# Hybrid encoder layer on one core: rows of 1 / rms spread inside the chip instead of through memory, the queries' row moved into the attention sigmoid

## The chip, the cores and the metric

The kernel runs on one core of one Trainium2 chip. The metric is the device time of one execution in microseconds (us). The kernel before was run three times: median 2429.84 us, from 2428.33 to 2432.44. The trace of before comes from a further, profiled execution of 2430.59 us.

## The reference, cut to what matters

One layer of a streaming encoder over 2048 prompt tokens and 64 sample tokens, model width 1024. `h = rms_norm(x)` goes through one input projection of 2048 columns. Part of them are queries and keys of 4 heads of 64:

```python
q = rms_norm(q.reshape(B, L, 4, 64), q_norm) * 64 ** -0.5
k = rms_norm(k.reshape(B, L, 4, 64), k_norm)
z = einsum("bqhd,bkhd->bhqk", q, k)              # stick-breaking attention
nl = where(mask, log1p(exp(z)), 0)               # 1 - sigmoid(z) = sigmoid(-z) survives
attn = where(mask, exp(z - surv), 0); o = attn @ v
x = x + concat(y_lru * gelu, y_pool, o) @ w_out
x = x + (silu(h2 @ w_gate) * (h2 @ w_up)) @ w_down    # h2 = rms_norm(x)
```

`rms_norm` multiplies each token (for q and k: each token and head) by one number, 1 / sqrt(mean of squares + eps), and each channel by a weight. The normalised keys are an output; the normalised queries are not.

## The kernel before, in words

The tokens are worked through in four groups of 512 (group 0 takes the 64 sample tokens along). Activations lie transposed: channels on the 128 partitions, tokens along the free axis. Every large product is done with operands split into a high and a low part (three matmuls). The split weights of the input projection are made in group 0, kept in memory (`wk`) and read back in groups 1 to 3.

`X_first` (L815) does the start: it loads x of group 0 and the values' weights, splits both, and computes the values' projection. In group 0 the rms factor is applied after the projection (`leave`, L305), from a tile `rb` in which every partition holds the row of 1 / rms over the tokens. The sums of squares come from matmuls with a column `ones`, which put them on the partitions (token = partition); GpSimd raises them to the power -0.5 (`inv_rms`, L138). To turn this column into a row on all partitions, before writes it to memory (`xrow`, L878) and reads it back broadcast to 128 partitions (L879). The sample tokens have their own write and read (L890, L891).

`QK_parts` (L326) treats one half (two heads, index j) of the queries or keys of one group in three steps: `mm_` projects into `raw` and squares it into `sq`; `ev_` sums the squares per head by matmuls with `sel`, takes the power -0.5 on GpSimd, writes the result to memory (`row`, L353; `rows` for the sample, L361) and reads it back broadcast into `rbk` (L356, L363); `fin_` multiplies `raw` by channel weight and `rbk` on VectorE (L368), splits it into `hl` (L314 on ScalarE, L315 on VectorE) and stores it for the attention (`qscr`, `kscr`). There are 16 such units: 4 groups, queries and keys, two halves. In the attention, `att_qtile` (L647) multiplies queries with keys into `z` and applies sigmoid with the scale -1 (L653), after which VectorE scans (L657, L661).

The order on each engine is set by a scheduler that simulates the program with its own costs; a string of tokens (`o0`, `o1`, `o3`) sets the order in which units are handed to it. Each engine then works strictly in its order, and so does SyncE's queue (SP), which issues every DMA: an issue that waits for a semaphore holds all behind it. `b_rbk` is 1: there is one `rbk` tile. `ps_mm` hands out three PSUM banks.

Of the kernel before, what the change touches and what calls it, by code (L numbers as in the profile page):

```python
# [3 lines left out]
def prm(n,d):  # L4
    return type(d)(PRM.get(n,d))
# [7 lines left out]
F32 = mybir.dt.float32  # L13
F32R = mybir.dt.float32r
# [7 lines left out]
P = 128  # L22
# [27 lines left out]
def hybrid_layer(ctx: ExitStack, tc: tile.TileContext, x_all, x_t, w_in, w_out, w_gu, w_dn, par, gates, poolw,  # L50
# [26 lines left out]
    def mm(out, lhsT, rhs, start, stop):  # L77
        pe.matmul(out, lhsT, rhs, start=start, stop=stop)  # L78
# [12 lines left out]
    qscr = [dram.tile([NH, HD, 2, GW], F32, name=f"qscr{g}") for g in range(NG)]  # L91
    qkrow = [[[dram.tile([2, GW], F32, name=f"row{g}{w}{j}") for j in range(2)] for w in range(2)] for g in range(NG)]
    qkrow_s = [[dram.tile([2, NS], F32, name=f"rows{w}{j}") for j in range(2)] for w in range(2)]
    mix = [dram.tile([KD, P, GW], F32, name=f"mix{g}") for g in range(NG)]
# [69 lines left out]
    def ps_t():  # L164
        return psum.tile([P, 4, P], F32, name="tp", tag="tp", bufs=prm("ntp", 2))
# [23 lines left out]
    qn8 = p1.tile([P, 1], F32, name="qn8")  # L189
    dve.tensor_scalar(qn8, pv("qn"), HD ** -0.5, None, ALU.mult)  # L190
    sel = p1.tile([P, 2], F32, name="sel")
# [113 lines left out]
    def leave(out, ps, g, a):  # L305
# [3 lines left out]
        else:  # L309
            act.copy(out, ps)  # L310

    def qk_split(raw, n):
# [5 lines left out]
    def q_store(hl, n, j, dst):  # L318
        for e in range(2):
            sp.dma_start(dst[2 * j + e], hl[e * HD:e * HD + HD, :, :n].bitcast(F32))  # L320

# [4 lines left out]
    def QK_parts(g, which, j):  # L326
# [11 lines left out]
        def ev_():  # L338
            raw, sq = st["raw"], st["sq"]
            ps = ps_st(prm('stt0', 0) if g == 0 else prm('stt', 0))  # L340
            rs = sm.tile([P, 10], F32, name="rs4")
            rs2 = sm.tile([P, 10], F32, name="rs42")
# [11 lines left out]
            rb = pq.tile([P, WM], F32, name="rbk", bufs=prm("b_rbk", 1))  # L354
            for e in range(2):
                sp.dma_start(rb[e * HD:e * HD + HD, :GW], row[e:e + 1, :].to_broadcast([HD, GW]))  # L356
            W = GW
            if g == 0:
                W = WM
                row = qkrow_s[which][j]  # L360
                sp.dma_start(row.rearrange("h p -> p h"), rs2[:NS, 8:10])  # L361
                for e in range(2):
                    sp.dma_start(rb[e * HD:e * HD + HD, GW:], row[e:e + 1, :].to_broadcast([HD, NS]))  # L363
            st["rb"] = rb, W

        def fin_():
            raw, (rb, W) = st["raw"], st["rb"]
            dve.scalar_tensor_tensor(raw[:, :W], raw[:, :W], qn8 if which == 0 else pv("kn"), rb[:, :W],  # L368
                                     ALU.mult, ALU.mult)
            for (a, n, t0, first) in [(0, GW, g * GW, True)] + ([(GW, NS, SEQ, False)] if g == 0 else []):  # L370
                hl = qk_split(raw[:, a:a + n], n)
                if which == 0:
                    q_store(hl, n, j, qscr[g] if first else qscr_s)
                else:
                    sp.dma_start(new_k[j * P:(j + 1) * P, t0:t0 + n], raw[:, a:a + n])
                    k_store(hl, n, j, kscr[g] if first else kscr_s[:, :, PAST:])

# [268 lines left out]

    def att_qtile(q2, n, K, w, dg, carry):  # L647

# [24 lines left out]
    def ATT_units(g):  # L673
        us = []
        for h in range(NH):
            st = {}
            for c in range(g, -1, -1):
# [11 lines left out]
                def u(pr, h=h, c=c, st=st, ld=ld):  # L689
# [33 lines left out]
    def ATT_sample(h):  # L723
# [9 lines left out]
        av = psum.tile([P, GW], F32, name="av", tag="av", bufs=1)  # L733
        at, _ = att_qtile(q2[:, :, :n], n, K, w, NS, 0.0)
        tp = ps_a()
# [79 lines left out]
    def X_first():  # L815
# [3 lines left out]
        for i in range(4):  # L819
# [10 lines left out]
            else:  # L830
# [5 lines left out]
        sp.dma_start(ident, ident_in)  # L836
        shift_consts()
        acc = [psum.tile([P, 512], F32, name=t, tag=t, bufs=b) for t, b in
               (("tp", prm("ntp", 2)), ("tp", prm("ntp", 2)), ("z", prm("nz", 2)), ("z", prm("nz", 2)), ("av", 1))]
# [28 lines left out]
        ps = ps_mm()  # L868
        rs = []
        rb = px.tile([P, WM], F32, name="rb", bufs=1)  # L870
        for o in (4, 0):
            for c in range(4):
                cs = slice(c * P, c * P + P) if o == 0 else slice(c, GW, 4)
                for e in range(2):
                    mm(ps[:, o + c:o + c + 1], sums[e][:, cs], ones, e == 0, e == 1)
            rs.append(inv_rms(sm, ps[:, o:o + 4], P, 4))
            if o:
# [10 lines left out]
        mm(ps[:NS, 8:9], ssm, ones, True, True)  # L888
        rss = inv_rms(sm, ps[:NS, 8:9], NS, 1)
        sp.dma_start(xrow[0][0:1, GW:].rearrange("o p -> p o"), rss[:NS, 0:1])  # L890
        sp.dma_start(rb[:, GW:], xrow[0][0:1, GW:].to_broadcast([P, NS]))  # L891
        for k in range(KD):
            mm3(acc[4][:NS, :256], hh_[:, k, GW:], hl_[:, k, GW:], W[k][0], W[k][1], k == 0, k == KD - 1)
        rb0.append(rb)
        for j, (ti, c0, n) in enumerate(toks(0)):
            with hp('ev'):
                ev_v(0, acc[j][:, :256], ti, c0, n, rss[:n, 0:1] if j == 4 else rs[1][:, j:j + 1])

# [478 lines left out]
```

## Time and profile before

| | |
|---|---|
| median of 3 runs | 2429.84 us |
| the profiled execution, its own time | 2430.59 us |
| its span, first to last instruction | 2428.8 us |
| TensorE (PE) busy | 2315.6 us, 95% |
| VectorE (DVE) busy | 1561.7 us, 64% |
| GpSimd (POOL) busy | 1112.7 us, 46% |
| ScalarE (ACT) busy | 965.6 us, 40% |
| mean granted TensorE clock | 0.975 of 2.4 GHz |
| PE busy from 1000 us to the end | 1408.05 of 1428.80 us |

The chain that ended last is 72% PE, 12% DVE, 9% DMA. A PE row counts records: a matmul of plain fp32 shows as two. In a timeline a piece has its start, its length, the engine, the line, what it writes and reads, and in brackets the idle time before it and what ended that.

### The profile page before, as it was taken

What the parts mean: (1) busy time and instruction counts of PE and PEld (TensorE: products, weight loads), DVE (VectorE), ACT (ScalarE), POOL (GpSimd) and SP (SyncE); (2) the same over time, 40 slices, a digit from 0 to 9 for tenths busy, and PEclk for the clock granted to TensorE, in tenths of its full rate; (3) what the DMA queues carried; (4) which work ended last, traced back from release to release, by engine and by line L of the source; (5) the groups of instructions that cost most, each with busy time, mean ns of one, the idle gap of its engine ahead of it and who ended that gap; (6) DMA issues with size and microseconds to landing.
All of it is one profiled execution on the core that took longest, in us unless ns stands there. A gap on an engine that the chain in (4) does not pass through costs nothing.

```text
span 2428.8 us, 38577 instructions
## 1 busy us (share of the span) xinstructions
PE 2315.6 (95%) x14230; PEld 2204.5 (91%) x14230; DVE 1561.7 (64%) x2514; ACT 965.6 (40%) x1804; POOL 1112.7 (46%) x818
## 2 busy tenths in 40 slices
PE   6987999999889989889999999999999999999999
PEld 6976778779678989889999999999999999999999
DVE  4568486796798644696676768655554655555455
ACT  4545364464565422233333343334333433333332
POOL 4533030131131133576565666656565765655552
PEclk8999999999999999999999999999999999999999
DMA  8986777656546354774343348633333563333332
GB/s 281 262 280 197 222 219 225 192 192 206 170 150 175 104 146 129 250 233 131 113 139 118 123 147 267 237 105 122 109 108 114 160 214 108 118 112 108 115 110 74
DMA packets 228478, 399.90 MB, mean 165 GB/s; under 512 B 37697, under 2 KB 99714, under 8 KB 220354
## 3 DMA queue, kind: packets, MB, share of 16 engines
q1 hardware_dynamic: 228290, 397.44, 52.6%
q8 instruction: 112, 1.84, 0.3%
q14 instruction: 76, 0.62, 0.1%
HBM read 300.81 MB, written 96.54 MB: 164 GB/s over the span
## 4 chain that ended last, share of the span: by engine, by line
PE 72%; DVE 12%; DMA 9%; issue 3%; ACT 2%; SPq 1%; POOL 1%; DVEq 0%; ACTq 0%; POOLq 0%
PE gu L78 33%; PE dn L78 20%; PE mm L78 14%; PE z L78 2%; PE av L78 2%; DVE C L661 1%; PE tp L705 1%; DMA rb<-xrow 1%; DMA kscr<-hl 1%; PE tp L78 1%; DVE xc L533 1%; DMA rbk<-row 1%; DMA x1all<-xr 1%; DMA wk<-w 1%; DVE al L1226 1%
## 5 line engine op out<-in xcount | busy, mean ns | idle before, releaser
L86 POOL TENSOR_TENSOR w<-x,w 128x512 fp32r<-128x512 f32 x462 | 640.7, 1401 | 509.7 <-ACT w L1103 478.4
L78 PE MATMUL dn<-ah,wd 128*128 128x352 f32 x2112 | 548.0, 324 | 5.4 <-ACT ah L1225 3.4
L78 PE MATMUL gu<-ht,w 128*128 128x352 f32 x2112 | 545.8, 323 | 7.3 <-DVE u L1180 7.1
L1103 ACT CAST w<-x 128x512 fp32r<-128x512 f32 x462 | 279.0, 619 | 521.2 <-PE gu L78 295.8
L78 PE MATMUL mm<-hTh,w 128*128 128x512 f32 (+3 forms) x1632 | 431.2, 342 | 13.7 <-DVE xr L1005 7.3
L78 PE MATMUL gu<-hb,w 128*128 128x352 f32 x1584 | 417.3, 325 | 9.0 <-DMA x<-in_w_gu 7.3
L1256 DVE TENSOR_TENSOR acc<-dn,acc 128x352 f32<-128x352 f32 x528 | 273.1, 522 | 217.5 <-PE dn L78 216.9
L78 PEld LDWEIGHTS dn<-ah,wd 128*128 128x128 f32 x2112 | 376.4, 189 | 7.6 <-ACT ah L1225 4.2
L78 PEld LDWEIGHTS gu<-ht,w 128*128 128x128 f32 x2112 | 375.1, 188 | 8.9 <-issue 5.9
L78 PE MATMUL dn<-al,wd 128*128 128x352 f32 x1056 | 342.4, 324 | 3.3 <-DVE al L1226 3.3
L78 PE MATMUL gu<-lt,w 128*128 128x352 f32 x1056 | 341.0, 323 | 0.0
L78 PEld LDWEIGHTS mm<-hTh,w 128*128 128x128 f32 x1632 | 290.2, 194 | 44.3 <-DVE xr L1005 8.5
L78 PEld LDWEIGHTS gu<-hb,w 128*128 128x128 f32 x1584 | 284.1, 189 | 11.1 <-ACT w L1103 9.5
L78 PE MATMUL mm<-hTl,w 128*128 128x512 f32 (+3 forms) x816 | 277.6, 341 | 0.8 <-DVE hTl L303 0.4
L78 PE MATMUL gu<-lb,w 128*128 128x352 f32 x792 | 257.1, 325 | 0.0
L86 POOL TENSOR_TENSOR wd<-x,wd 128x512 fp32r<-128x512 f32 x132 | 192.4, 1478 | 51.6 <-ACT wd L1244 51.6
L78 PEld LDWEIGHTS dn<-al,wd 128*128 128x128 f32 x1056 | 199.7, 189 | 4.5 <-DVE al L1226 4.5
L78 PEld LDWEIGHTS gu<-lt,w 128*128 128x128 f32 x1056 | 198.6, 188 | 0.0
L78 PEld LDWEIGHTS mm<-hTl,w 128*128 128x128 f32 x816 | 157.8, 193 | 15.7 <-issue 1.4
L661 DVE TENSOR_TENSOR_SCAN C<-z,C,zero 128x512 f32<-128x512 f32 (+4 forms) x148 | 160.6, 1087 | 13.9 <-ACT z L653 7.5
L1180 DVE TENSOR_TENSOR u<-gu,u 128x352 f32<-128x352 f32 x132 | 68.9, 522 | 129.1 <-PE gu L78 128.8
L78 PEld LDWEIGHTS gu<-lb,w 128*128 128x128 f32 x792 | 150.0, 189 | 0.0
(272 smaller groups left out, 3540.5 us busy)
## 6 DMA issues: line engine op xcount, KB each, us to landing
x<-in_w_gu SPq DMA_DIRECT2D x220, 256.0 KB, 3.3
w<-wk SPq DMA_DIRECT2D x46, 1024.0 KB, 5.7
x<-wsc SPq DMA_DIRECT2D x176, 256.0 KB, 3.4
x<-in_w_dn SPq DMA_DIRECT2D x132, 256.0 KB, 2.8
wsc<-x SPq DMA_DIRECT2D x88, 256.0 KB, 2.7
wk<-w SPq DMA_DIRECT2D x16, 1024.0 KB, 9.1
V<-vscr SPq DMA_DIRECT2D x40, 256.0 KB, 3.8
K<-kscr SPq DMA_DIRECT2D x40, 256.0 KB, 3.6
```

Source lines behind the costliest of these rows:

```text
L78: pe.matmul(out, lhsT, rhs, start=start, stop=stop)
L86: gp.tensor_tensor(out, src, hi, ALU.subtract)
L533: dve.scalar_tensor_tensor(xc[:, a:b], xa[:, s + j:s + j + b - a], pv("cw", c * 4 + j), xc[:, a:b], ALU.mult, ALU.add)
L661: dve.tensor_tensor_scan(C[:n, :w][:, ::-1], om[:n, :w][:, ::-1], zero1[:n].to_broadcast([n, w]), carry, ALU.mult, ALU.add)
L705: pe.transpose(tp[:, kt, :], at[:, kt * P:(kt + 1) * P], ident)
L1103: act.copy(w[:, 0, :], src)
L1180: add = lambda o, x, y: dve.tensor_tensor(o, x, y, ALU.add)
L1226: dve.tensor_tensor(al[:, cs], o, ah[:, cs], ALU.subtract)
L1256: dve.tensor_tensor(acc[:, d, a:b], ps[:, :HT], acc[:, d, a:b], ALU.add)
```

## The change

Queries are no longer multiplied by their 1 / rms. The split `hl` of a query is made from `raw` times the channel weight (now with a minus sign) directly; the 1 / rms of the query tokens, which the power leaves on partitions, is kept in the tiles `qrs`, and the attention's sigmoid takes it as a scale per partition instead of the constant -1. Keys and the rms of group 0 still need a row on all partitions: `rows` transposes the 8 columns of 1 / rms on PE to 8 rows, ScalarE copies these to SBUF, and `spread` makes the row on all 128 partitions by four fp32 matmuls with a table of ones and zeros (`pick`), into PSUM, where VectorE reads it for the keys (for group 0, ScalarE copies it into `rb`). The tokens of a sum of squares are taken in blocks of 128 instead of every fourth one. All writes and reads of `row`, `rows` and, for group 0, `xrow` are gone.

```diff
@@ X_first and QK_parts share:
+    def rows(r, smp, tp=None):
+        tp = ps_t().rearrange("p a b -> p (a b)") if tp is None else tp
+        rt = sm.tile([8, P + NS], F32, name="rt", bufs=2)
+        pe.transpose(tp[:8, :P], r[:, :8], ident)
+        act.copy(rt[:, :P], tp[:8, :P])
+        if smp:
+            pe.transpose(tp[:2, P:P + NS], r[:NS, 8:10], ident[:NS, :NS])
+            act.copy(rt[:2, P:], tp[:2, P:P + NS])
+        return rt
+    def spread(rt, ps):
+        for t in range(4):
+            mm(ps[:, t * P:t * P + P], pick[:, t, :], rt[:, :P], True, True)
@@ ev_ of QK_parts
-                mm(ps[:, t:8:4], sq[:, t:GW:4], sel, True, True)
+                mm(ps[:, t:8:4], sq[:, t * P:t * P + P], sel, True, True)
...
-            row = qkrow[g][which][j]
-            sp.dma_start(row.rearrange("h (p t) -> p h t", t=4), rs2[:, :8].rearrange("p (h t) -> p h t", t=4))
...
-                sp.dma_start(rb[e * HD:e * HD + HD, :GW], row[e:e + 1, :].to_broadcast([HD, GW]))
...
+            if which:
+                st["rt"] = rows(rs2, g == 0)
@@ fin_ of QK_parts
-            dve.scalar_tensor_tensor(raw[:, :W], raw[:, :W], qn8 if which == 0 else pv("kn"), rb[:, :W],
-                                     ALU.mult, ALU.mult)
...
+            if which == 0:
...
+                    act.activation(hl[:, 0, :n], r, AF.Copy, scale=qn8)
+                    dve.scalar_tensor_tensor(hl[:, 1, :n], r, qn8, hl[:, 0, :n], ALU.mult, ALU.subtract)
...
+                    ps = ps_mm()
+                    spread(st["rt"], ps)
+                dve.scalar_tensor_tensor(r, r, pv("kn"), ps[:, :n], ALU.mult, ALU.mult)
+                hl = qk_split(r, n)
@@ att_qtile
-        act.activation(om[:n, :w], z[:n, :w], AF.Sigmoid, scale=-1.0)
+        act.activation(om[:n, :w], z[:n, :w], AF.Sigmoid, scale=rs)
@@ X_first
-        for o in (4, 0):
...
-                sp.dma_start(xrow[0][0:1, :GW].rearrange("o (p t) -> (o p) t", t=4), rs[0][:, :4])
-                sp.dma_start(rb[:, :GW], xrow[0][0:1, :GW].to_broadcast([P, GW]))
+        for c in range(4):
+            for e in range(2):
+                mm(ps[:, c:c + 1], sums[e][:, c * P:c * P + P], ones, e == 0, e == 1)
...
+        rbp = ps_mm()
+        spread(rows(rs, False, ps[:, P:]), rbp)
+        act.copy(rb[:, :GW], rbp)
```

How the change moves instructions, at three places. First PE right after the sums of squares in `X_first` (`w_604` and `w_598` are the weights of the first query half; `rsx` is the column of 1 / rms, `rt` its transposed rows). Before:

```order
L78 MATMUL mm<-ones,r 128x1
L78 MATMUL mm<-ones,i 128x1
L78 MATMUL mm<-hTh,w_604 128x288
L78 MATMUL mm<-hTl,w_604 128x288
L78 MATMUL av<-w_247,hTh 64x256 x2
```

Now, some rows further:

```order
L78 MATMUL av<-w_314,hTl 64x256
L326 MATMUL mm<-ident,rsx 8x128
L453 MATMUL tp<-ident,vf 128x128 x4
L78 MATMUL mm<-rt,pick 128x128 x4
L78 MATMUL mm<-ones,ssm 64x1
L78 MATMUL mm<-hTh,w_598 128x288
L78 MATMUL mm<-hTl,w_598 128x288
```

The transposition and the four spreading matmuls now stand ahead of the first query projection, which before stood behind the sums; the second set of sums, which followed it, is gone.

Second, SP's queue around the first query half's row (`row_69`, `rows_85`). Before:

```order
L353 DMA row_69<-rs_730 128x2x4
L361 DMA rows_85<-rs_730 64x2x1
L283 DMA xt<-in_x_all 128x1024 x2
L430 DMA vtscr_95<-vT 128x2x128
L293 DMA xrow_104<-rs_3005 128x4
L446 DMA vf<-in_cache_v 128x256 x2
L223 DMA stg<-in_w_in 128x1024
L409 DMA vscr_61<-vs 128x512
L356 DMA rbk<-row_69 64x512 x2
L363 DMA rbk<-rows_85 64x64 x2
```

Now, at the same place:

```order
L227 DMA stg<-in_w_in 128x1024
L236 DMA wk_0_1049<-w_1044 128x2048
L390 DMA qscr_65<-hl 64x1024 x2
L457 DMA vtscr_75<-vT 128x2x128
L287 DMA xt<-in_x_all 128x1024 x2
```

The write and the reads of the row are gone, and the store of the split query stands where the row's write stood.

Third, PE in group 1 at the keys of group 2 (`pick` again the table, `rs_4151` and `rs_4221` the two halves' columns). Before:

```order
L78 MATMUL mm<-sel,sq 128x2 x4
L78 MATMUL mm<-xc,pw 128x512
L705 MATMUL tp<-ident,C 128x128
L78 MATMUL tp<-vf,dm 128x256
L78 MATMUL tp<-vf,em 128x256
```

Now:

```order
L733 MATMUL tp<-ident,C 128x128 x4
L326 MATMUL tp<-ident,rs_4151 8x128
L78 MATMUL av<-aTh,V 128x256
L733 MATMUL tp<-ident,C 128x128 x4
L78 MATMUL mm<-rt,pick 128x128 x4
L78 MATMUL mm<-xc,pw 128x512
L78 MATMUL mm<-sel,sq 128x2 x4
```

One matmul and four transpositions stand between the transposition of the keys' row and the matmuls that spread it, which need ScalarE's copy of it.

## Rows read from the trace of the kernel before

**Rows 1.** Stages: window, length, busy us PE, PEld, DVE, ACT, POOL; clock; DMA share; GB/s.

```profile
30.00:60.00 30.00, 19.60 (x129) 17.97 (x128) 2.78 (x12) 8.83 (x19) 10.49 (x7) 0.78 0.97 293
90.00:120.00 30.00, 30.00 (x189) 27.65 (x188) 20.79 (x44) 13.68 (x24) 20.27 (x12) 0.94 0.99 258
120.00:150.00 30.00, 23.98 (x136) 21.29 (x136) 19.96 (x37) 13.37 (x22) 9.16 (x6) 0.83 0.85 239
```

**Rows 2.** PE timeline, first stall: start, length, what; idle before it and releaser.

```profile
49.87 0.78 PE L78 MATMUL tp<-vf,dm 128*128 128x256 f32 x2 [3.00 <-ACT vT L428]
53.39 0.66 PE L426 MATMUL tp<-ident,vf 128*128 128x128 f32 x2 [1.89 <-DVE vs L408]
59.56 0.61 PE L78 MATMUL mm<-hTh,w 128*128 128x288 f32 x1 [5.51 <-DVE raw L308]
```

**Rows 3.** SP timeline, group 0's row of 1 / rms, and the chain's piece of it.

```profile
31.27 1.45 SPq L878 DMA_DIRECT2D xrow<-rs  x1
48.64 0.32 SPq L879 DMA_DIRECT2D rb<-xrow  x1
...
48.64 10.39 DMA rb<-xrow
```

**Rows 4.** Stages after two stalls, same columns as rows 1.

```profile
59.50:64.00 4.50, 4.44 (x18) 4.44 (x19) 0.83 (x3) 2.60 (x5) 0.00 (x0) 0.50 1.03 325
130.00:140.00 10.00, 4.46 (x9) 2.78 (x10) 7.90 (x10) 6.52 (x12) 7.00 (x5) 0.61 0.82 255
```

**Rows 5.** DMA in group 0: packets of 104 to 120 us; stages, last columns share and GB/s.

```profile
DMA packets 1675, 2.78 MB, mean 174 GB/s; under 512 B 1036, under 2 KB 1036, under 8 KB 1546
...
60.00:76.00 16.00, 16.00 (x88) 15.50 (x88) 2.94 (x8) 9.84 (x19) 4.66 (x3) 0.77 1.01 362
76.00:87.00 11.00, 11.00 (x83) 10.90 (x82) 4.71 (x11) 5.57 (x12) 4.48 (x3) 1.00 1.04 148
108.00:120.00 12.00, 12.00 (x93) 12.00 (x92) 11.97 (x22) 3.27 (x6) 9.70 (x5) 1.00 0.96 110
```

**Rows 6.** Timelines of DVE (first row) and PE, second stall.

```profile
130.09 2.88 DVE L368 SCALAR_TENSOR_TENSOR raw<-raw,qn,rbk 128x576 f32<-128x576 f32 x1 [6.23 <-DMA rbk<-rows]
133.38 1.33 PE L78 MATMUL mm<-xc,gw 128*128 128x288 f32 x2 [3.49 <-DVE sqt L308]
136.87 2.29 PE L78 MATMUL mm<-xc,gw 128*128 128x288 f32 x4 [2.15 <-DVE sqt L308]
```

**Rows 7.** PE timeline, waits for group 2's and group 3's own keys.

```profile
457.04 0.73 PE L78 MATMUL z<-K,q 128*128 128x128 f32 x4 [1.65 <-DMA K<-kscr]
659.22 1.01 PE L78 MATMUL z<-K,q 128*128 128x128 f32 x3 [4.32 <-DMA K<-kscr]
```

**Rows 8.** PE timeline, sums of squares: weights of consecutive columns, then of every fourth.

```profile
34.45 0.28 PE L78 MATMUL mm<-ones,r 128*128 128x1 f32 x2
...
36.15 0.43 PE L78 MATMUL av<-w,hTh 128*64 128x256 f32 x2
...
67.68 2.02 PE L78 MATMUL z<-sel,sq 128*128 128x2 f32 x10
69.64 0.40 PE L78 MATMUL mm<-hTh,w 128*128 128x288 f32 x1
```

**Rows 9.** PE timeline, two transpositions and one fp32 matmul of 256 columns.

```profile
41.20 0.38 PE L426 MATMUL tp<-ident,vf 128*128 128x128 f32 x2
260.02 0.60 PE L78 MATMUL tp<-vf,dm 128*128 128x256 f32 x2
```

**Rows 10.** Groups of ACT by shape, up to 1000 us: count, busy us, mean ns, idle before.

```profile
L653 ACT ACTIVATE z<-z 128x512 f32<-128x512 f32 x112 | 65.4, 586 | 32.5 <-PE z L78 26.1 <-issue 5.0 <-ACT z L653 0.3
L558 ACT ACTIVATE r<-mm,par_sb 128x512 f32<-128x512 f32 x12 | 8.2, 680 | 5.3 <-PE mm L78 3.0 <-issue 1.3 <-DMA mix<-r 1.0
```

**Rows 11.** Groups of DVE and POOL by shape, up to 900 us, same columns.

```profile
L661 DVE TENSOR_TENSOR_SCAN C<-z,C,zero 128x512 f32<-128x512 f32 x96 | 122.2, 1275 | 13.2 <-ACT z L653 7.5 <-PE tp L705 4.8
L315 DVE TENSOR_TENSOR hl<-raw,hl 128x512 fp32r<-128x512 f32 x16 | 11.0, 686 | 10.4 <-ACT hl L314 10.3
...
L351 POOL TENSOR_TENSOR rs<-rs,mhalf 128x8 f32<-128x8 f32 x16 | 27.3, 1704 | 145.3 <-DVE rs L350 145.3
```

More of the change, by code (lines that the diff above doesn't have):

```diff
@@ L91, in hybrid_layer @@
     qscr = [dram.tile([NH, HD, 2, GW], F32, name=f"qscr{g}") for g in range(NG)]
-    qkrow = [[[dram.tile([2, GW], F32, name=f"row{g}{w}{j}") for j in range(2)] for w in range(2)] for g in range(NG)]
-    qkrow_s = [[dram.tile([2, NS], F32, name=f"rows{w}{j}") for j in range(2)] for w in range(2)]
     mix = [dram.tile([KD, P, GW], F32, name=f"mix{g}") for g in range(NG)]
@@ L189, in hybrid_layer @@
     qn8 = p1.tile([P, 1], F32, name="qn8")
-    dve.tensor_scalar(qn8, pv("qn"), HD ** -0.5, None, ALU.mult)
+    dve.tensor_scalar(qn8, pv("qn"), -HD ** -0.5, None, ALU.mult)
+    qrs = [[p1.tile([P, 10], F32, name=f"qrs{i}{j}") for j in range(2)] for i in range(2)]
+    pick = p1.tile([8, 4, P], F32, name="pick")
+    picks = p1.tile([2, P], F32, name="picks")
     sel = p1.tile([P, 2], F32, name="sel")
@@ L310, in leave, with pick_consts, spread_s @@
             act.copy(out, ps)
+    def pick_consts():
+        for e in range(2):
+            es = slice(e * HD, e * HD + HD)
+            for t in range(4):
+                dve.tensor_copy(pick[:, t, es], ident[:8, 4 * e + t:4 * e + t + 1].to_broadcast([8, HD]))
+            dve.tensor_copy(picks[:, es], ident[:2, e:e + 1].to_broadcast([2, HD]))
+    def rows(r, smp, tp=None):
[8 more added lines that the diff above has]
+    def spread(rt, ps):
+        for t in range(4):
+            mm(ps[:, t * P:t * P + P], pick[:, t, :], rt[:, :P], True, True)
+    def spread_s(rt, ps):
+        mm(ps[:, :NS], picks, rt[:2, P:], True, True)
     def qk_split(raw, n):
@@ L341, in ev_ @@
             rs = sm.tile([P, 10], F32, name="rs4")
-            rs2 = sm.tile([P, 10], F32, name="rs42")
+            rs2 = qrs[g % 2][j] if which == 0 else sm.tile([P, 10], F32, name="rs42")
             for t in range(4):
-                mm(ps[:, t:8:4], sq[:, t:GW:4], sel, True, True)
+                mm(ps[:, t:8:4], sq[:, t * P:t * P + P], sel, True, True)
             parts = [(P, 0, 8)]
@@ L351, in ev_ @@
                 gp.tensor_tensor(rs2[:n, a:b], rs[:n, a:b], mhalf[:n, 0:1].to_broadcast([n, b - a]), ALU.pow)
-            row = qkrow[g][which][j]
-            sp.dma_start(row.rearrange("h (p t) -> p h t", t=4), rs2[:, :8].rearrange("p (h t) -> p h t", t=4))
-            rb = pq.tile([P, WM], F32, name="rbk", bufs=prm("b_rbk", 1))
-            for e in range(2):
-                sp.dma_start(rb[e * HD:e * HD + HD, :GW], row[e:e + 1, :].to_broadcast([HD, GW]))
[L357 to L363, printed above, removed]
@@ new lines, in fin_ @@
+        def fin_():
+            raw = st["raw"]
+            parts = [(0, GW, g * GW)] + ([(GW, NS, SEQ)] if g == 0 else [])
+            if which == 0:
+                for (a, n, t0) in parts:
+                    r = raw[:, a:a + n]
+                    hl = pq.tile([P, 2, GW], F32R, name="hl", bufs=prm("b_hl", 1))
+                    act.activation(hl[:, 0, :n], r, AF.Copy, scale=qn8)
+                    dve.scalar_tensor_tensor(hl[:, 1, :n], r, qn8, hl[:, 0, :n], ALU.mult, ALU.subtract)
+                    dst = qscr_s if a else qscr[g]
+                    for e in range(2):
+                        sp.dma_start(dst[2 * j + e], hl[e * HD:e * HD + HD, :, :n].bitcast(F32))
+                return
+            for (a, n, t0) in parts:
+                r = raw[:, a:a + n]
+                if a:
+                    ps = ps_t().rearrange("p a b -> p (a b)")
+                    spread_s(st["rt"], ps)
+                else:
+                    ps = ps_mm()
+                    spread(st["rt"], ps)
+                dve.scalar_tensor_tensor(r, r, pv("kn"), ps[:, :n], ALU.mult, ALU.mult)
+                hl = qk_split(r, n)
+                sp.dma_start(new_k[j * P:(j + 1) * P, t0:t0 + n], r)
+                k_store(hl, n, j, kscr_s[:, :, PAST:] if a else kscr[g])
@@ L868, in X_first @@
         ps = ps_mm()
-        rs = []
         rb = px.tile([P, WM], F32, name="rb", bufs=1)
-        for o in (4, 0):
[L872 to L877, printed above, removed]
-                sp.dma_start(xrow[0][0:1, :GW].rearrange("o (p t) -> (o p) t", t=4), rs[0][:, :4])
-                sp.dma_start(rb[:, :GW], xrow[0][0:1, :GW].to_broadcast([P, GW]))
+        rsq = sm.tile([P, 10], F32, name="rs4")
+        rs = sm.tile([P, 10], F32, name="rsx", bufs=1)
+        for c in range(4):
+            for e in range(2):
+                mm(ps[:, c:c + 1], sums[e][:, c * P:c * P + P], ones, e == 0, e == 1)
+        for e in range(2):
+            dve.tensor_scalar(rsq[:, 4 * e:4 * e + 4], ps[:, :4], 1.0 / D, EPS, ALU.mult, ALU.add)
+        gp.tensor_tensor(rs[:, :8], rsq[:, :8], mhalf[:, 0:1].to_broadcast([P, 8]), ALU.pow)
+        rbp = ps_mm()
+        spread(rows(rs, False, ps[:, P:]), rbp)
+        act.copy(rb[:, :GW], rbp)
         sg = pl.tile([P, SW], F32, name="xa", tag="xa", bufs=LB["xa"])[:, :GW].rearrange("p (k t) -> p k t", k=KD)
@@ L888, in X_first @@
         mm(ps[:NS, 8:9], ssm, ones, True, True)
-        rss = inv_rms(sm, ps[:NS, 8:9], NS, 1)
-        sp.dma_start(xrow[0][0:1, GW:].rearrange("o p -> p o"), rss[:NS, 0:1])
-        sp.dma_start(rb[:, GW:], xrow[0][0:1, GW:].to_broadcast([P, NS]))
+        for e in range(2):
+            dve.tensor_scalar(rsq[:NS, 8 + e:9 + e], ps[:NS, 8:9], 1.0 / D, EPS, ALU.mult, ALU.add)
+        gp.tensor_tensor(rs[:NS, 8:10], rsq[:NS, 8:10], mhalf[:NS, 0:1].to_broadcast([NS, 2]), ALU.pow)
+        tp = ps[:, P:]
+        rt = sm.tile([8, P + NS], F32, name="rt", bufs=2)
+        pe.transpose(tp[:2, P:P + NS], rs[:NS, 8:10], ident[:NS, :NS])
+        act.copy(rt[:2, P:], tp[:2, P:P + NS])
+        spread_s(rt, rbp)
+        act.copy(rb[:, GW:], rbp[:, :NS])
         for k in range(KD):
@@ L896, in X_first @@
             with hp('ev'):
-                ev_v(0, acc[j][:, :256], ti, c0, n, rss[:n, 0:1] if j == 4 else rs[1][:, j:j + 1])
+                ev_v(0, acc[j][:, :256], ti, c0, n, rs[:n, 8:9] if j == 4 else rs[:, j:j + 1])
     X_first()
```

19 lines of the change are left out of this document (5 added, 14 removed).

## The prediction, word for word
> **What bounds the kernel now.** I read the page first: PE is busy for 95% of the span and the chain that ended last is 72% PE, so the time is PE's work plus the places where PE stands still or runs at the lower clock. Next I read the stages. From 1000 us on, in the part that the change does not touch, PE is busy for 1408.05 of 1428.80 us. The idle time lies early: 10.4 us in 30 to 60 us and 6.0 us in 120 to 150 us, while between them PE is busy throughout [rows 1]. Then I asked the PE timeline what ended each pause.
>
> In the first pause PE finds three things missing one after the other, 3.00 + 1.89 + 5.51 us [rows 2]. The last and longest is ended by VectorE's multiplication with `rb`. SP tells why that was late: the write of the row was issued at 31.27 us, its read back only at 48.64, and the read took 10.39 us to land [rows 3]. Behind the pause PE's granted clock is 0.50 for 4.5 us, the lower of its two levels [rows 4].
>
> In the second pause VectorE had stood idle for 6.23 us for `rbk`, the second query half's row; the gelu evacuations (`sqt`) queued behind it, and PE waited for these for 3.49 + 2.15 us. The mean clock of 130 to 140 us is 0.61 [rows 4, 6].
>
> The DMA rows show what makes these trips slow. All of group 0 has a DMA share near 1. Where large pieces move, the rate is 362 GB/s; in 76 to 87 and 108 to 120 us the share is the same and the rate 148 and 110 GB/s [rows 5]. In 104 to 120 us there are 1036 packets under 512 B. By their shapes in SP's order, one row write is 128 x 2 pieces of 16 B and the sample's is 64 x 2 pieces of 4 B, 384 together; two such pairs are 768 of the 1036.
>
> **The change, part by part.** Terms are on PE's path, against the profiled execution of 2430.6 us (0.75 us above the median).
>
> *Removed: group 0's trip through memory.* The new chain starts at the same sums, which end near 29.5 us: GpSimd's power (1.70 us by the row of 8 columns [rows 11]), a transposition (0.19 us, half of a pair [rows 9]), ScalarE's copy behind three others (four of at most 0.59 us [rows 10], 2.4), four matmuls (1.2, or 2.4 at the lower clock), and the copy to `rb` (0.6) behind work of some 1.5 us. That is about 9 us, so `rb` stands near 38 us and not at 59. Before, PE used the wait to do projection that it does now as well, so what is gained is the pause: **-10.4 us** (bounds -12.4 and 0; the upper one if something else keeps PE waiting, see the rivals). The lower clock behind it goes too: half of 4.5 us, **-2.2**.
>
> By the Trainium skill (DMA: Bandwidth & Descriptors, section Latency and other measured facts) the fixed cost of a DMA is about 2 us, mostly the access to memory; two of them, write and read, would be some 4 us, and the first term an estimated -4 instead of -10.4. The trace does not agree: the read alone took 10.39 us, in a queue share of 0.97 [rows 1, 3].
>
> *Removed: `rbk`.* Queries wait for no row at all any more, keys for PE only. Of the second pause I take all 5.64 us, and half of the 4.46 busy us at the low clock as the loss there, less what other idle time would have cost: **-7.3** (bounds -8 and -2, since the gelu chain itself has some us of waits). The waits for group 2's and 3's own keys, 1.65 + 4.32 us [rows 7], end when a key has gone through row, store and load; one of three trips is gone. I take half, **-3** (bounds -6 and 0).
>
> *Weights of the sums.* Before, a sum of squares loads every fourth column of `sq` as weights: ten records from 67.68 to 69.64 us, 0.196 us each, of which two were consecutive already. The sixteen records with consecutive columns take 34.45 to 36.15, 0.106 us each [rows 8]. Both stretches are at full clock. 16 units x 8 records x 0.09 = 11.5 us, and the second set of sums (the 1.70 us) is gone: **-13.2** (bounds -13.2 and -1.7, if the stride isn't what makes the difference).
>
> *Added on PE.* Each of 8 key units and group 0 has a transposition (0.19) and four fp32 matmuls of 128 columns. One of 256 columns takes 0.60 us [rows 9]; two weight loads of 0.106 are the floor of one of 128, so one costs 0.21 to 0.60, and I take 0.30, half of the nearest row. 9 x (0.19 + 1.2) = 12.5, and the sample's three small sets 1.4: **+13.9** (bounds 9.5 to 25). Weights and spreading so cancel: +0.7 together.
>
> *The sigmoid's scale.* A sigmoid with constants takes 586 ns for 512 columns, one with an operand per partition 680 [rows 10]; the trace has 164 of the former (112 of this shape, 48 smaller, 4 of the sample), so 15.4 us of ScalarE's time. ScalarE is busy 40%; what counts is where VectorE's scan waits for it, 7.5 us in all before the large scans [rows 11]. I take **+2** (bounds 0 and 15.4).
>
> *New waits.* Transposition and matmuls now stand in PE's own queue and wait for GpSimd and ScalarE; all of PE's work stands behind them. In two of the three later groups, for two halves each, only a few short rows lie between the transposition and the matmuls that need its copy. One ScalarE instruction in the way is 0.6 us, so four times that, and a little for the other two: **+3** (bounds 0 and 38, see the rivals).
>
> *VectorE and queues.* A query loses one pass of 0.686 us, 8 times 5.5 us [rows 11]; VectorE is not the bound where it stands, so I count **-1**. The keys' product reads PSUM now, at nothing: PE's matmuls cover VectorE's reads. SP loses 64 issues. The small writes' DMA time in group 0, about (1 - 148/362) x 11 + (1 - 110/362) x 12 = 15 us, is worth nothing by itself, but it is the room in which weights can follow a PE that is ahead.
>
> Sum: -10.4 - 2.2 - 7.3 - 3 + 0.7 + 2 + 3 - 1 = -18.2 us, so 2412.4 for the profiled execution and **2412** on the median's level.
>
> **The rivals.** *DMA keeps the old pace* (0.14). Group 0 runs at DMA share 0.97 to 1; if the weights, the kept copies and the x loads come no sooner, PE is ahead only to wait for `w`. Then the first two terms and most of the second pause go, and about -6 is left: 2424. For it speaks the share; against it the 15 us of small packets that vanish, and 362 GB/s where they are absent.
>
> *More than the pauses* (0.13). With the DMA free, the other idle and low-clock time of group 0 shrinks too. PE's idle in 120 to 150 us is 6 us [rows 1], all its low clock could go, and the key waits in full: up to -33, 2397.
>
> *PE's queue is held by the small steps* (0.07, slower). Place: the 8 key units. If nothing useful stands between sum, transposition and spreading, each unit pays power 1.70, a scan ahead of VectorE's step 1.28, transposition 0.2, two ScalarE instructions 1.2 and the step's own 0.3: 4.7 us, 8 x 4.7 = 38 in place of 3, so 2447. It decides from (18.2 + 3) / 8 = 2.6 us a unit. Against it: some ten or more rows lie between sums and transposition in the new order, by the simulated costs.
>
> *The sigmoids are all on the path* (0.04): +15.4 instead of +2 leaves -5, 2425. The Trainium skill (ScalarE: Activation LUTs, section What ACT_TABLE_LOAD costs) gives about 93 ns for each operand per partition; the trace's 94 agrees.
>
> *The edit doesn't do what it says*: the new order shows the rows' writes and reads gone, so no chance is left for that.
>
> **How the numbers follow.** The forecast has 0.62, with its own range 2402 to 2421. About 0.2%, 5 us, is what a measurement of this kernel can tell from no change. Faster: 0.62 + 0.13 + 0.10 of the slow-DMA case = 0.85. Same: the rest of that case and the sigmoids, 0.08. Slower: 0.07. The range reaches from the second rival to the first and the fourth, 2395 to 2427.
>
> **What would show it.** In the profile after: no pause over 3 us between 40 and 62 us, and `rb` copied near 38 us; no VectorE wait for a row near 130; rates over 250 GB/s all through group 0; records of `sel,sq` near 0.11 us; the end of group 0's projections some 15 to 20 us before the present 174. I am wrong if PE waits for `w` in 50 to 150 us, if `rt,pick` shows waits over 2.6 us a unit, or if idle time ended by VectorE's scan grows by more than 5 us.

## The result, and the profile after

The changed kernel takes 2449.05 us (median of 6 runs, 2445.2 to 2455.25), the kernel before 2429.09 in the same series: ratio 1.0081, 95% interval [1.0065, 1.0098]. It is slower by 20 us where 18 us less were forecast. The profiled execution took 2449.94 us, with a span of 2448.2 us and a mean clock of 0.976.

The stages of the kernel after, same columns as [rows 1], the first three for the same stretches:

```profile
30.00:60.00 30.00, 29.61 (x203) 28.22 (x204) 7.56 (x26) 15.11 (x32) 13.14 (x8) 0.90 0.89 310
90.00:120.00 30.00, 21.77 (x96) 17.78 (x97) 11.13 (x26) 7.82 (x17) 10.51 (x6) 0.60 0.82 280
120.00:150.00 30.00, 29.56 (x208) 27.25 (x207) 21.68 (x42) 15.66 (x29) 14.45 (x10) 1.00 0.72 228
...
690.00:800.00 110.00, 93.13 (x553) 75.08 (x552) 103.90 (x137) 70.58 (x116) 21.77 (x12) 0.95 0.41 119
800.00:1010.00 210.00, 197.54 (x1510) 195.26 (x1510) 81.77 (x147) 55.77 (x120) 65.22 (x79) 0.94 0.47 139
```

The first pause is gone: 29.61 busy us in 30 to 60 where before had 19.60. But 90 to 120 us, full before, now has 8.2 us of idle time and a mean clock of 0.60. What was won is paid back 40 us later. The PE timeline of that place:

```profile
87.61 0.29 PE L78 MATMUL mm<-hTh,w 128*128 128x288 f32 x1
90.83 1.11 PE L78 MATMUL tp<-vf,dm 64*64 64x256 f32 x2 [2.93 <-ACT vT L455]
91.87 1.11 PE L78 MATMUL tp<-clast,e 1*64 1x256 f32 x2
93.27 1.19 PE L78 MATMUL tp<-vf,dm 128*128 128x256 f32 x2 [0.29 <-DMA vf<-in_cache_v]
101.14 1.22 PE L78 MATMUL tp<-vf,dm 128*128 128x256 f32 x2 [6.67 <-DVE vs L435]
102.15 1.06 PE L78 MATMUL tp<-vf,em 128*128 128x256 f32 x2
103.00 0.42 PE L326 MATMUL tp<-ident,rs 128*8 128x128 f32 x1
103.86 0.26 PE L329 MATMUL tp<-ident,rs 64*2 64x64 f32 x1 [0.44 <-ACT rt L327]
104.05 2.07 PE L78 MATMUL mm<-rt,pick 8*128 8x128 f32 x8
106.06 0.61 PE L78 MATMUL mm<-hTh,w 128*128 128x288 f32 x1
```

From the end of one projection at 87.9 to the start of the next at 106.06 PE has nothing but small steps: the shift of cached values, then the key's transposition and its spreading. The names behind the idle times (ScalarE's `vT`, VectorE's `vs`) belong to the cached values; the chain there goes on over GpSimd, where a weight split of 2.34 us stood ahead. Of the key's own chain only ScalarE's copy `rt` shows, with 0.44 us. But a late small step costs PE nothing as long as a projection can run meanwhile. The question of the experiments is why none does.

Other rows answer to those of before. VectorE's wait for `rbk` [rows 6] is gone with the row. The ten records of a sum take 0.109 us each (1.09 / 10) where they took 0.196 [rows 8], as priced. `rb` is copied at 37.94 us, as foretold. The key units' transpositions wait for GpSimd's power twice in groups 1 to 3, for 1.9 us in all. The PE timeline of after, at a sum and at the two transpositions that wait:

```profile
82.09 1.16 PE L78 MATMUL z<-sel,sq 128*128 128x2 f32 x10
83.18 0.40 PE L78 MATMUL mm<-hTh,w 128*128 128x288 f32 x1
...
425.35 0.27 PE L326 MATMUL tp<-ident,rs 128*8 128x128 f32 x1 [0.59 <-POOL rs L375]
...
609.18 0.38 PE L326 MATMUL tp<-ident,rs 128*8 128x128 f32 x1 [1.27 <-POOL rs L375]
```

The second place is late. Stage 690 to 800 lost 8 us of PE's time against before, where it read:

```profile
690.00:800.00 110.00, 101.13 (x718) 91.10 (x717) 98.40 (x138) 67.86 (x124) 24.07 (x17) 0.97 0.57 169
```

The scores and the output projection of the kernel before, by tile (durations min/median/max in ns, first and last start in us, shapes):

```profile
L78 PE MATMUL z<-K,q x328: 220/396/793, 173.8 to 828.1; 128*128 128x512 f32 x112, 128*128 128x128 f32 x16, 128*128 128x256 f32 x16, 128*128 128x384 f32 x16
L78 PE MATMUL mm<-hTh,woh x256: 274/283/581, 721.7 to 990.9; 128*128 128x256 f32 x112, 128*128 128x320 f32 x16
```

The same of the kernel after:

```profile
L78 PE MATMUL z<-K,q x328: 220/395/792, 146.2 to 790.1; 128*128 128x512 f32 x112, 128*128 128x128 f32 x16, 128*128 128x256 f32 x16, 128*128 128x384 f32 x16
L78 PE MATMUL mm<-hTh,woh x256: 278/283/582, 792.8 to 1009.9; 128*128 128x256 f32 x112, 128*128 128x320 f32 x16
```

Before, the output projection ran beside the last 106 us of the attention. After, it begins 2.7 us behind the attention's last score. The chain of waits of after (start, length, what) shows the attention alone with VectorE's scan as its pace, and then weights, splits and inputs one after the other:

```profile
786.70 1.27 DVE C L688
...
788.47 1.28 DVE C L688
789.75 0.04 issue
789.79 0.53 PE z L78 x2
790.32 2.45 DMA q<-vtscr
792.77 2.38 POOL wol L86
795.17 3.48 DMA stg<-in_w_out
798.65 0.02 issue
798.67 1.05 ACT woh L1007
```

### The profile page after: what moved, and what is told of

Its sections match the earlier page's. It is cut to its first block, busy times and chain, and to the rows that moved or that the text cites. A ratio compares the mean times of both kernels' runs of the same rounds, so it can differ in the third digit from the quotient of the medians.

```text
span 2448.2 us, 38637 instructions
## 1 busy us (share of the span) xinstructions
PE 2323.2 (95%) x14304; PEld 2198.8 (90%) x14304; DVE 1559.8 (64%) x2519; ACT 982.1 (40%) x1818; POOL 1104.6 (45%) x817
## 4 chain that ended last, share of the span: by engine, by line
PE 70%; DVE 13%; DMA 8%; issue 3%; POOL 2%; ACT 2%; SPq 1%; DVEq 0%; POOLq 0%; ACTq 0%
PE gu L78 31%; PE dn L78 19%; PE mm L78 15%; DVE C L688 3%; DMA x1all<-xr 2%; PE z L78 1%; PE av L78 1%; PE tp L733 1%; DVE aTl L735 1%; POOL w L86 1%; DVE xc L560 1%; PE tp L78 1%; DMA x<-in_w_dn 1%; DMA x<-in_w_gu 1%; DMA stg<-mix 1%
```

## The experiments

All versions, in us; the ratio is to the kernel before, run beside them.

| version | median | ratio, 95% interval |
|---|---|---|
| the change | 2449.05 | 1.0081 [1.0065, 1.0098] |
| e1: queries' rows outlive the stage | 2437.03 | 1.0033 [1.0015, 1.0051] |
| e2: before, -1 in a tile of the stage's pool | 2458.98 | 1.0126 [1.0106, 1.0145] |
| e3: before, -1 in a tile that outlives it | 2440.64 | 1.0042 [1.0026, 1.0058] |
| e4: before, first rows only | 2427.45 | 0.9991 [0.9978, 1.0004] |
| e15: e4 and -1 in a tile that outlives it | 2426.59 | 0.9978 [0.9966, 0.9990] |
| e7: e1, queries by memory, plain sigmoid | 2450.77 | 1.0075 [1.0058, 1.0092] |
| e6: e1, keys by memory | 2401.08 | 0.9882 [0.9867, 0.9898] |
| e12: e6, rows in the stage's pool | 2423.11 | 0.9970 [0.9955, 0.9985] |
| e8: e1, queries spread too, plain sigmoid | 2475.86 | 1.0187 [1.0169, 1.0205] |
| e10: e1, spread rows in a tp tile | 2406.61 | 0.9900 [0.9882, 0.9917] |
| e10z: e1, spread rows in a z tile | 2409.29 | 0.9910 [0.9890, 0.9931] |
| e13: e8, spread rows in a tp tile | 2425.01 | 0.9980 [0.9968, 0.9992] |
| e9: e4, splits on GpSimd | 2416.34 | 0.9943 [0.9926, 0.9959] |
| e11: e6, splits on GpSimd | 2392.70 | 0.9842 [0.9821, 0.9863] |
| e14: e10, splits on GpSimd | 2395.87 | 0.9855 [0.9838, 0.9872] |

**A tile that is read after its stage.** `qrs` comes from the pool `p1`, which the program closes ahead of the output projection; the attention reads it to its end. Theory: what takes over the pool's memory waits for that read. e1 moves the tile, e2 and e3 put such a tile into the kernel before, and e12 tries it again without the keys' spreading.

```diff
 e1 (e12 undoes it in e6)
-    qrs = [[p1.tile([P, 10], F32, name=f"qrs{i}{j}") for j in range(2)] for i in range(2)]
+    qrs = [[cp.tile([P, 10], F32, name=f"qrs{i}{j}") for j in range(2)] for i in range(2)]
 e2 (e3: cp.tile)
+    neg1 = p1.tile([P, 1], F32, name="neg1")
+    gp.memset(neg1, -1.0)
...
-        act.activation(om[:n, :w], z[:n, :w], AF.Sigmoid, scale=-1.0)
+        act.activation(om[:n, :w], z[:n, :w], AF.Sigmoid, scale=neg1[:n])
```

> The changed kernel with one edit: the tiles that hold the queries' 1/rms come from the pool that lives to the end, not from the stage's pool that is closed ahead of the output projection. Theory A (the attention's reads of these tiles keep the closed pool's memory occupied, so the output projection cannot start until the last sigmoid, and the attention's tail runs alone): 2412 to 2428 us, the first output-projection matmul more than 40 us ahead of the last query-key product, and no stretch of 40 us in which VectorE is busy over 90% and PE under 85%. Theory B (the small steps for the keys hold PE's queue): 2446 to 2452, as the changed kernel. Theory C (the operand of the sigmoid lengthens the attention's chain): 2446 to 2452.

> The kernel before with one edit: the sigmoid's scale -1 is read from a tile of ones times -1 in the stage's pool; rows, keys and queries go through memory as before. Theory A: 15 to 35 us slower than before (2444 to 2464), the output projection starting only behind the last query-key product, as in the changed kernel. Theory B: as before, within 3 us. Theory C: 2 to 15 us slower, equal to the next run.

> The same with the tile in the pool that lives to the end. Theory A: 2429 to 2433, a sigmoid of 512 columns taking 680 ns and not 586. Theory B: as before, within 3 us. Theory C: 2434 to 2444, equal to the run with the stage's pool.

> The changed kernel with the keys' rows alone taken back to memory: the queries' rows stay in the stage's pool. Lifetime theory (the output projection waits for the attention's last read of that pool): 12 to 18 us above the same kernel whose rows outlive the stage (2401), so 2412 to 2420 us. If the lifetime only mattered beside the keys' spreading: 2398 to 2406.

Three pairs differ in the pool alone: 2449.05 to 2437.03, 2458.98 to 2440.64, and 2423.11 to 2401.08: 12, 18 and 22 us, all one way. The rows by tile show the mechanism each time, here in e12:

```profile
L78 PE MATMUL z<-K,q x328: 218/396/803, 173.0 to 768.5; 128*128 128x512 f32 x112, 128*128 128x128 f32 x16, 128*128 128x256 f32 x16, 128*128 128x384 f32 x16
L78 PE MATMUL mm<-hTh,woh x256: 279/283/582, 771.2 to 990.9; 128*128 128x256 f32 x112, 128*128 128x320 f32 x16
```

And in e6:

```profile
L78 PE MATMUL z<-K,q x328: 220/396/792, 175.0 to 799.1; 128*128 128x512 f32 x112, 128*128 128x128 f32 x16, 128*128 128x256 f32 x16, 128*128 128x384 f32 x16
L78 PE MATMUL mm<-hTh,woh x256: 274/283/416, 690.0 to 965.6; 128*128 128x256 f32 x112, 128*128 128x320 f32 x16
```

In e12 the output projection begins 2.7 us after the last score, in e6 109 us before it. The programs show the same: in each pair PE's order is the same, over more than 3300 matmuls, up to the point where the version whose tile outlives the stage has its first matmul of the output projection; and in the changed kernel the copy that makes the first `woh` waits for the last sigmoid that reads `qrs`, which in e1 it does not. The theory stands, though only e2 fell into its range: e1 came out 9 us above it, e3 8 and e12 3. So it does not account for all: e1 is still 7 us above before, and e3, which only takes the -1 from a tile, 10 us. I took these 10 us for the price of the sigmoid's operand.

**First rows, and the operand.** e4 is the kernel before with the new `X_first` alone; e15 adds e3's two lines to it.

> The kernel before with the change of X_first alone (transposition and spreading for the rms of group 0; queries and keys through memory, the sigmoid's constant). If the first pause was worth what the forecast counted: 2416 to 2421, with PE busy for more than 28 of 30 us in 30 to 60 us. If other work of group 0 only waits later (the DMA's pace, the cached values): 2426 to 2432.

> The kernel before with the first group's part (2427 us), and the sigmoid's scale of -1 taken from a tile that outlives the stage. If the operand itself costs, as 664 ns where the constant takes 586 ns: 2433 to 2441, about 10 us more, as over the kernel before. If those 10 us were the order's: anything else, most likely 2422 to 2431.

e4 equals before. Its first projection of 512 columns starts at 177.9 us (before 187.8) and its last at 673.3 (687.4), but its attention's last score at 824.9 (828.1) and its feed-forward part at 996.3 (998.7). So the pause of group 0 was worth 10 us where it lay and 2 at the end. On the way PE, being ahead, meets a wait of another kind, by waits in 90 to 190 us of e4 (total, times, longest):

```profile
ACT w L227 <- DMA stg<-in_w_in: 14.3, 4, 6.1
...
PE mm L78 <- ACT hTh L304: 11.9, 1, 11.9
```

e15 is no slower than e4, although each of its sigmoids takes as long as the change's (112 of 512 columns; in [rows 10] 586 ns):

```profile
L681 ACT ACTIVATE z<-z,neg 128x512 f32<-128x512 f32 x112 | 73.8, 663 | 27.2 <-PE z L78 23.1 <-issue 1.4 <-ACT vf L447 1.0
```

So the operand theory falls: the 77 ns are there, and in the kernel's time they don't show. For e3's 10 us the other order is left, in which the scheduler then put the rest (PE's order in e3 departs from before's after 877 of 14042 matmuls). That the order is the cause isn't shown by a run of its own, but I take it that an edit of this size can move this kernel by some 10 us.

**Which part costs.** e6 takes the keys' rows back to memory, e7 the queries' (with the plain sigmoid); e8 spreads the queries on PE as well.

```diff
 e6: ev_ of the keys writes row and reads rbk as before, their sums take every fourth token again; fin_ of the keys
+            dve.scalar_tensor_tensor(raw[:, :W], raw[:, :W], pv("kn"), rb[:, :W], ALU.mult, ALU.mult)
...
-                    spread(st["rt"], ps)
-                dve.scalar_tensor_tensor(r, r, pv("kn"), ps[:, :n], ALU.mult, ALU.mult)
 e7: the same for the queries with qn8; e7 and e8
-        act.activation(om[:n, :w], z[:n, :w], AF.Sigmoid, scale=rs)
+        act.activation(om[:n, :w], z[:n, :w], AF.Sigmoid, scale=-1.0)
 e8: queries spread as keys
-            if which:
-                st["rt"] = rows(rs2, g == 0)
+            st["rt"] = rows(rs2, g == 0)
...
-                dve.scalar_tensor_tensor(r, r, pv("kn"), ps[:, :n], ALU.mult, ALU.mult)
+                dve.scalar_tensor_tensor(r, r, pv("kn") if which else qn8, ps[:, :n], ALU.mult, ALU.mult)
```

> The changed kernel, with the queries' 1 / rms taken back to memory and to a row that DVE multiplies in, and with the sigmoid's scale a constant -1 again (so no tile of the stage's pool is read by the attention); keys and first group as in the change. Operand theory (the sigmoid's scale per partition, 664 ns for 128x512 where the constant takes 586 ns, costs about 10 us): 2420 to 2430 us, level with the kernel with the first group's rows alone (2427). If the loss that remained when the rows outlived the stage (2437) came from the keys' transpositions and fp32 matmuls: 2434 to 2442.

> The changed kernel with the queries' rows outliving the stage, and the keys' 1 / rms taken back to memory. Operand theory: the 78 ns per sigmoid stay, so 2434 to 2444 us, as with the keys spread (2437). If the keys' spreading is what costs: 2424 to 2431.

> The changed kernel with the queries' 1 / rms spread by a transposition and four fp32 matmuls as the keys' are, multiplied in by DVE, and a constant -1 in the sigmoid: nothing goes by memory, no tile of the stage's pool is read by the attention, no operand in the sigmoid. Operand theory: 2422 to 2431 us (the eight query units take some 8 us of matmuls more, partly in idle time). If the spreading by small matmuls is what costs: above 2437, since there is twice as much of it.

All three missed the operand theory's figures, e6 and e7 the other range as well, and together they turn it round. Against the median of before beside them, 2430.40 us, the kernel with the operand and without the keys' spreading is 29 us faster (e6), the one with the keys' spreading and no operand 20 us slower (e7), and the one with twice the spreading 45 us slower (e8). So the queries' part is a gain (e4 to e6: 26 us; e7 to e1, beside the keys' spreading: 14), and the keys' spreading costs 36 us (e6 to e1). Its instructions cannot: eight records of a spread take 1.15 us at full clock, and there are eight key units, which makes some 9 us. In e8 the stages name a place; 60 to 90 us of it:

```profile
60.00:90.00 30.00, 12.36 (x41) 7.11 (x39) 5.11 (x11) 13.54 (x28) 8.15 (x5) 0.56 0.90 306
```

**The turn of the PSUM tiles.** The spread rows are written to a tile `mm`, one of three that the projections use in turn. The next projection then gets a tile that comes after the spread's in that turn. PE's order in the changed kernel, where the first key unit of group 0 ends (rows with the same operands are merged and numbered):

```
286 L78 MATMUL mm<-hTh,w_1044 128x288
287 L78 MATMUL tp<-vf,dm 64x256
288 L78 MATMUL tp<-clast,e_190 64x256
289 L78 MATMUL tp<-vf,dm 128x256 x2
290 L78 MATMUL tp<-vf,em 128x256
291 L326 MATMUL tp<-ident,rs_1015 8x128
292 L329 MATMUL tp<-ident,rs_1015 2x64
293 L78 MATMUL mm<-rt,pick 128x128 x4
294 L78 MATMUL mm<-hTh,w_1140 128x288
```

The projection of `w_1140` stands right behind the spread, and so behind sum, power, transposition and copy. e10 gives the spread a tile of the transpositions, e10z one of the scores, e13 does e10's edit in e8.

```diff
 e10, e13 (e10z: ps_st(2))
-                    ps = ps_mm()
+                    ps = ps_t().rearrange("p a b -> p (a b)")
                     spread(st["rt"], ps)
```

> The changed kernel with the queries' rows outliving the stage (2437 us), and with the keys' spread rows written to a PSUM tile of the transpositions (tag tp) and not to one of the three that the projections use in turn (tag mm). Turn theory (the spread's place in that turn puts transposition and spread on PE ahead of the next projection, which then waits for sums, DVE, GpSimd and ACT): 2400 to 2420 us, near the kernel with the keys' rows by memory (2401). If the spreading's own instructions are what costs: 2432 to 2442, no change.

> As the kernel before it, with the spread rows in a PSUM tile of the attention's scores (tag z). Turn theory: 2400 to 2425 us; it may come out above the one with tag tp, since the scores have two such tiles and the attention's next score then waits for DVE's product. If the spreading's own instructions cost: 2432 to 2442.

> Keys and queries spread by PE, both into a PSUM tile of the transpositions, and a plain constant in the sigmoid; with the projections' tiles the same kernel took 2476 us. Turn theory: most of those 70 us come back, 2405 to 2425. Against the version whose queries' rows go by the sigmoid's operand (2407): if the operand costs 10 us and the spreading of eight query units 8, the two are level, 2402 to 2410; if the operand costs next to nothing: 2412 to 2425.

In e10's order `w_1140` follows row 286 at once, and this spread comes at row 400, over a hundred rows later. Up to this projection the orders of e1, e10 and e10z are the same, matmul for matmul; here they first part. Same instructions, same data: e1 to e10 is 30 us, to e10z 28, e8 to e13 51 (e13 on the upper edge of its range). Of the 30 us of e1 to e10, 25 are there by the end of group 0. The first projection of group 1 in e1, then in e10:

```profile
188.61 1.22 PE L78 MATMUL mm<-hTh,w 128*128 128x512 f32 x2 [0.71 <-ACT hTh L306]
```

```profile
163.92 1.22 PE L78 MATMUL mm<-hTh,w 128*128 128x512 f32 x2 [2.76 <-ACT hTh L306]
```

Two stages of e10:

```profile
90.00:120.00 30.00, 30.00 (x205) 27.28 (x204) 18.58 (x46) 17.45 (x34) 16.79 (x10) 1.00 1.00 336
120.00:150.00 30.00, 30.00 (x221) 29.04 (x220) 23.78 (x53) 10.72 (x22) 13.08 (x8) 1.00 0.73 261
```

And its PE timeline, the spread in its new place:

```profile
110.48 1.72 PE L78 MATMUL mm<-xc,gw 128*128 128x288 f32 x6
112.13 1.15 PE L78 MATMUL tp<-rt,pick 8*128 8x128 f32 x8
```

The pause of 88 to 106 us is gone and the clock stays at its upper level. The theory stands. It says what holds the next projection back; what PE then waits for there are, by the rows above, the cached values, whose steps come ahead of the transposition in PE's order. e13 against e10 gives a price besides: spreading the queries too costs 18 us more than the operand. And e6 beats e10 by 5.5 us: for the keys, memory is as good once their spread no longer stops PE.

**Late work on VectorE.** e4 left open where its 10 us went. From 690 to 800 us VectorE is the busiest engine after PE (95.64 of 110 us in e4). Theory: it sets the end of the attention, and taking work from it helps. e9, e11 and e14 move one line, the low halves of the output projection's inputs (32 instructions, 12 of them between 690 and 830 us in e4), to GpSimd.

```diff
-              dve.tensor_tensor(hl_[:, js, off:off + n], ms[:, :, :n], hh_[:, js, off:off + n], ALU.subtract)
+              gp.tensor_tensor(hl_[:, js, off:off + n], ms[:, :, :n], hh_[:, js, off:off + n], ALU.subtract)
```

> The kernel before with the first group's part alone (2427 us: its projections ended 10 to 14 us sooner, its attention only 3 us sooner), and with the low halves of the output projection's inputs (12 to 14 subtractions of 0.72 us between 690 and 830 us) moved from DVE to GpSimd. Late-DVE theory (between the projections' end and the attention's end DVE, busy 26 to 28 of 30 us, sets the time, so that what the first group gains waits there): 2418 to 2424 us. If DVE is not what sets the end there: 2425 to 2431, the same as without.

> The kernel with the keys' rows by memory and the queries' rows outliving the stage (2401 us), and the low halves of the output projection's inputs on GpSimd. Late-DVE theory: 8 to 12 us less, 2389 to 2394. If DVE is not the limit once the attention ends sooner: 2397 to 2402.

> The changed kernel with all three mended: the queries' rows outlive the stage, the keys' spread rows in a PSUM tile of the transpositions, and the low halves of the output projection's inputs on GpSimd. Late-DVE theory: 8 to 12 us below the version without the last (2407), so 2395 to 2399. If DVE no longer sets the end there: 2403 to 2408.

11.1, 8.4 and 10.7 us less; e11 and e14 are within what was expected, and e9 came out 2 us below its range. The work is the same and takes longer on GpSimd. The group of e4, 690 to 830 us, then that of e9:

```profile
L990 DVE TENSOR_TENSOR hTl<-stg,hTh 128x512 fp32r<-128x512 f32 (+1 forms) x12 | 8.8, 747 | 0.7 <-ACT hTh L988 0.6
```

```profile
L990 POOL TENSOR_TENSOR hTl<-stg,hTh 128x512 fp32r<-128x512 f32 (+1 forms) x12 | 16.5, 1379 | 28.7 <-ACT hTh L988 28.4
```

The stages of e4, and below them those of e9:

```profile
690.00:800.00 110.00, 99.97 (x731) 92.77 (x730) 95.64 (x131) 61.57 (x117) 17.91 (x16) 0.97 0.52 152
800.00:1010.00 210.00, 189.94 (x1429) 186.23 (x1429) 101.50 (x168) 65.97 (x135) 67.22 (x76) 0.96 0.48 145
```

```profile
690.00:800.00 110.00, 103.22 (x748) 94.66 (x749) 93.88 (x130) 65.64 (x123) 31.72 (x25) 0.98 0.55 161
800.00:1010.00 210.00, 194.82 (x1481) 192.12 (x1480) 94.98 (x156) 67.92 (x141) 100.21 (x102) 0.97 0.54 158
```

PE gained 3.3 us in the first stage and 4.9 in the second, so the line paid behind the attention as well. Each gain is of the size that I put down to an order above; three of them, all one way, are what speaks for VectorE's late work. That just the 10 us of group 0 wait there is not shown, since the line was not moved in the kernel before alone. e11, at 0.9842 [0.9821, 0.9863], is the fastest version: first rows and queries as in the change, queries' rows outliving the stage, keys by memory, splits on GpSimd.

## Why the prediction was wrong

**The step that failed is *New waits*.** It looked for waits of the small steps themselves, inside the later groups, and put +3 us on them. Those waits were that small (1.9 us for GpSimd in groups 1 to 3). What the step left out are two waits of what comes after them: the projection that stands behind the spread, in PE's order, by its turn of a PSUM tile (30 us, e1 to e10), and the output projection that waits for a pool's memory until the attention has read `qrs` (12 us, after to e1). Together 42 us. Without the two the same edit takes 2406.61 us, inside the forecast's own range of 2402 to 2421. That is luck in part: the sum had -12.6 for group 0's trip, which alone brings nothing that can be told from no change (e4), and -10.3 for `rbk`, where the queries' part alone brought 14 to 26.

A count over the trace says in what form they came. For each window of 10 us up to the first matmul of the feed-forward part I add PE's idle time, and PE's busy time times 2 x (1 - mean clock), an estimate of the time at the lower level. Work is the rest, with half of the low time taken off:

| | feed-forward begins | idle | low clock | work |
|---|---|---|---|---|
| before | 998.7 | 92.0 | 72.3 | 870.6 |
| after | 1017.4 | 100.9 | 79.6 | 876.7 |
| e1 | 1004.4 | 89.2 | 88.7 | 870.9 |
| e10 | 975.1 | 73.1 | 68.4 | 867.8 |
| e6 | 973.0 | 83.3 | 53.0 | 863.2 |

Between e1 and e10 idle time falls by 16.1 us and half the low time by 10.2, which is 26.3 of the 29.3; PE's work hardly differs. From before to after the 19 us are 9 of idle time, 4 of the clock and 6 of work. The column of idle time also shows what the prediction's reading passed over: its two pauses are 16 us, and of before's 92.0 us of idle time 57 lie behind 200 us.

**Removed: group 0's trip.** Right as to the pause (29.61 busy us, `rb` at 37.94) and its 10 us at the place, wrong as to the end. Alone it brings nothing that can be told from no change (e4), so the upper bound of 0 held, not the -10.4. In the changed kernel the pause at 88 to 106 us takes it back within group 0.

**Removed: `rbk`.** Too small, as far as the queries go: -7.3 and -3 were for queries and keys together, and the queries' part alone, with half of the contiguous sums, is 26 us (e4 to e6), or 14 where the keys are spread (e7 to e1). I have not taken this apart further.

**Weights of the sums, added on PE.** Both sizes held (0.109 us a record; 1.15 us for four matmuls where 1.2 was taken), and they nearly cancel: work is 870.6 before, and 867.8 to 876.7 in the three versions with both.

**The sigmoid's scale.** +2 was taken between 0 and 15.4, and nothing of it can be told in the time (e15 against e4: 2426.59 and 2427.45). ScalarE's operation does take longer; by the changed kernel's groups

```profile
L680 ACT ACTIVATE z<-z,qrs 128x512 f32<-128x512 f32 x112 | 74.2, 664 | 39.3 <-PE z L78 35.1 <-PE tp L733 2.7 <-DVE aTl L735 0.8
```

which is 78 ns more, where the Trainium skill's 93 (ScalarE: Activation LUTs, section What ACT_TABLE_LOAD costs) was cited in the prediction with 94 from another form.

**The rivals.** *PE's queue is held by the small steps* named the engine and almost the number (2447). Its mechanism, 4.7 us in every key unit, is not what happened: no transposition in groups 1 to 3 waits for GpSimd longer than 1.27 us, and one place in group 0 alone has 8.2 us of idle time at a clock of 0.60. My reason against it, "some ten or more rows lie between sums and transposition", was read in a later group; in group 0 some twenty rows of projection do stand there, and then the small steps with no projection left. The question should have been what stands behind the spread. *DMA keeps the old pace* stays open for e4 and does not show in the changed kernel: PE's 11.9 us in e4 are ended by ScalarE's `hTh`, which waits for VectorE there, and the 14.3 us in which ScalarE waits for weights are not PE's. *The sigmoids are all on the path*: no.

**What would show it.** Two of the good signs failed: the rate is 228 GB/s in 120 to 150 us, and the last projection of group 0 starts at 174.9 us, where before had it at 174.3 (e10: 148.6). Of the three conditions for being wrong none was met: PE waits nowhere for `w` in 50 to 150 us, no wait at `rt,pick` comes near 2.6 us, and PE's idle time ended by VectorE's scan is 17.7 us (18.2 before). They asked for the waits that the sum had named, and the 6.67 us at 101.14 end at another VectorE step, the split of the cached values.

## What to carry to other kernels

A tile ties together two lives that the arithmetic doesn't: whoever takes one of the tiles that a loop uses in turn puts that loop's next step behind his own chain, and whoever reads a tile after its stage holds back what takes over the stage's memory. So ask of each added operand which pool it is from, who takes its next turn and who follows in its memory, and look in the order at what stands right behind the new steps. And where a scheduler writes the order, test a cause in two settings: a two-line edit was worth +10 us in one and nothing in the other.

## What the runs showed that was not expected

- The pauses of 88 to 101 us in the changed kernel are followed by a stretch at the lower clock: the stage of 90 to 120 us is 21.77 us busy at a mean of 0.60. Between e1 and e10 the clock makes 10 of 29 us.
- VectorE's split of 0.75 us, given to GpSimd at 1.38 us, made the kernel 8 to 11 us faster three times over.
- Writing rows of 1 / rms to memory and reading them back is not slow in itself: for the keys it is no worse than transposing and spreading them, even with the spread well placed (2401.08 and 2406.61, less apart than the 10 us put down to an order).
- By the Trainium skill (Perfetto Trace Analysis, section Optimization Strategy) the same gap repeating on the engine that should be saturated can mean that there is no room for the next tile. Here it was the turn of a PSUM tile that was wrong, not room: the gaps don't repeat, each names another engine as its end, and no row of waits names the tile.
